# Two raw halves of a gate weight: landing place and place in the load queue

## The chip, the cores and the metric

The kernel runs on one core of a Trainium2 chip. A core has five engines that work side by side, each through its own instructions in order: TensorE (PE, matmuls), VectorE (DVE), ScalarE (ACT), GpSimd (POOL) and SyncE (SP, which here issues nearly all DMAs). They wait for each other through semaphores. The metric is the device time of one execution in microseconds, as the median of several runs.

## The reference, cut to what matters

One layer of an encoder: 1024 tokens of 1024 channels. The normalized input `h` is projected to queries, keys and values for two attention branches and to 2048 gate columns; each branch is projected to 1024 channels, gated, merged and projected again, and a SwiGLU block follows. The part of interest is the gate projection, and the last two units of the neighbourhood attention beside it:

```python
proj = h @ w_in[l]
qa, ka, va, qb, kb, vb, gates = jnp.split(proj, split_at, axis=-1)
...
o_a = neighbourhood_attention(qa, ka, va, rpb[l])
...
gate_a, gate_b = jnp.split(jax.nn.sigmoid(gates + b_gate[l]), 2, axis=-1)
merged = gate_a * (o_a @ w_proj_a[l]) + gate_b * (o_b @ w_proj_b[l])
```

## The kernel before

**Splitting.** Matmuls of float32 quality are made of three passes. `wsplit` (L125) makes a rounded upper part `whi` on ACT (L129) and the rest `wlo` on POOL or DVE (L130); each product then takes `whi` with both parts of the other operand and `wlo` with the upper part (`PASS`, L148).

**The gate products.** The gate columns are cut into eight weights `i`, each with four quarters of 128x512 (`q` = 0 to 3; in the text 5q3 is quarter 3 of weight 5). Products of 2x2 blocks are saved by mixing: with quarters w11, w12, w21, w22 (`q` 0 to 3), `x1 = w21 + w22`, `x2 = x1 - w11` and `x4 = w12 - x2` are formed on DVE (L761, L763, L768) and multiplied with mixed blocks of `h` that were prepared earlier. Weights go in pairs, `GPAIRS` = (5,6), (7,2), (0,1), (3,4), through four phases w11, w12, x1, x4 (`GPHASE`). One phase of one pair fills one slot `n` of the main loop: pair (5,6) the slots 80 to 83, pair (7,2) from 84 on. A phase has eight chunks of three matmuls (L773): four for the first weight of the pair, then attention work of the slot (scores L502, value products L543, transposes L528), then four for the second weight. What a product gives is drained from its `ps_d` bank, of which there are two, by L779 or L781 into `ga` and `gc` tiles and stored to DRAM (L808).

**Preparing a pair.** `gate_prep(p, part)` runs in the slots of `GPREP`: (0, 0) in slot 77, (0, 1) in slot 79. Part 0 splits quarters 0 and 1, part 1 mixes. Pairs behind the first are loaded whole by `gate_load` (L740) into a tile that a unit's queries and keys leave free. For the first pair no such tile is free, and its eight quarters go one by one through `wload` (L118) into the `raw` landing tiles of 128x512, of which there are six (`NRAW`). Quarters 0 and 1 of both weights hold four of them until they are mixed; the other two pass through the combine steps (`ut`, L677, read at L709 and L711).

**What sets the order.** PE's order is the program's. On ACT, DVE, POOL and SP a planner places the instructions: it simulates the program in time and takes, of what is ready, the first by program order, so DVE and the others then run in a fixed order on the chip. A tile with several buffers takes whichever is free in that simulation. `pin` (L113) keeps an instruction behind the one that was traced before it on its engine. `wload` with `keep` is pinned: in part 1 the loads of weight 6 are so pinned behind the store of weight 5's `x2` (L765).

**The attention tiles.** `big` (L162) gives one of eight tiles of 128x1024 (`NBIG`). At this point of the program they hold the bias tables of units 8 and 9 (two each, L449, read at L516), the values `v` of a unit (L378, loaded at L392), the weights of the conditioning rows (L296, read at L322), the accumulator `oacc` (L676, stored at L1104) and the gate's `gc` (L799).

```python
754                     gwt[i, nm] = wsplit(graw[i, q])
...
757         for i in pr:
758             for q in (2, 3) if p == 0 else ():
759                 graw[i, q] = gate_raw(i, q)
760             r = [graw.pop((i, q)) for q in range(4)]
761             nc.vector.tensor_add(r[2], r[2], r[3])
762             gwt[i, "x1"] = wsplit(r[2])
```

Of the kernel before, what the change touches and what calls it, by code (L numbers as in the profile page):

```python
# [48 lines left out]
def hybrid_layer(ctx: ExitStack, tc: tile.TileContext, x, colp, wada1, wada2, bada2, wqkv, wg, wpa, wpb,  # L49
                 wo, w1, w2, hgain, ropeg, rope, rbias, bmask, g2r, out):  # L50
    nc = tc.nc
# [61 lines left out]
    pin = tc.keep_in_program_order  # L113
# [4 lines left out]
    def wload(src, n, keep=False):  # L118
        raw = wp.tile([128, 512], F32, tag="raw", bufs=NRAW, name="raw")
        d = nc.sync.dma_start(raw[:, :n], src)  # L120
        if keep:
            tc.keep_in_program_order(d)
        return raw[:, :n]

    def wsplit(r, eng=None):  # L125
        n = r.shape[1]
        hi = wp.tile([128, 512], F32R, tag="hi", bufs=NHL, name="whi")
        lo = wp.tile([128, 512], F32R, tag="lo", bufs=NHL, name="wlo")
        nc.scalar.activation(hi[:, :n], r, AF.Copy)  # L129
        (eng or nc.gpsimd).tensor_sub(lo[:, :n], r, fview(hi[:, :n]))  # L130
        return hi, lo
# [30 lines left out]
    def big(name, shape=None, dtype=F32):  # L162
        return ap_.tile(shape or wide, dtype, tag="big", bufs=NBIG, name=name)
# [561 lines left out]
    gwt, gacc, gbank, graw, glate = {}, {}, {}, {}, {}  # L725
# [11 lines left out]
    def gate_raw(i, q):  # L737
        return wload(wg[i, :, 4 * q:4 * q + 4, :], 512, True)
# [8 lines left out]
    def gate_prep(p, part):  # L747
        pr = GPAIRS[p]
        if part == 0:
            for i in pr if p == 0 else ():  # L750
                for q in (0, 1):
                    graw[i, q] = gate_raw(i, q)
            for nm, q in (("w11", 0), ("w12", 1)):
                for i in pr:
                    gwt[i, nm] = wsplit(graw[i, q])
            return
        for i in pr:
            for q in (2, 3) if p == 0 else ():
                graw[i, q] = gate_raw(i, q)
            r = [graw.pop((i, q)) for q in range(4)]  # L760
            nc.vector.tensor_add(r[2], r[2], r[3])  # L761
            gwt[i, "x1"] = wsplit(r[2])
            nc.vector.tensor_sub(r[2], r[2], r[0])  # L763
            if p < 3:
                nc.sync.dma_start(sig_d[i, 4], r[2])  # L765
            else:
                glate[i] = r[2], r[3]
            nc.vector.tensor_sub(r[1], r[1], r[2])  # L768
            gwt[i, "x4"] = wsplit(r[1], nc.vector)
# [236 lines left out]
    for n in range(6, 92):  # L1006
# [92 lines left out]
        if n in GPREP:  # L1099
            gate_prep(*GPREP[n])  # L1100
# [152 lines left out]
    for i in GPAIRS[3]:  # L1253
        gacc[i] = [sig_half()]
        sig[i, 0, 0] = gacc[i][0]
        gate_acc(i, False)
    gate_prep(3, 1)
    cover("w11")
    mixed_load("x2")
# [493 lines left out]
```

## Time and profile before

| | |
|---|---|
| median of 3 runs | 1496.59 us (1496.54 to 1497.46) |
| the profiled execution | 1494.47 us |
| its span, first to last instruction | 1492.7 us |
| mean granted clock of TensorE | 0.998 |
| HBM read, written | 184.06 MB, 64.86 MB |

The profile is of one execution. Its page gives the busy time of each engine, and the trace behind it answers finer questions: who waited for whom, a timeline of each engine, busy time and granted clock in a stretch. In a timeline row stand the start, the duration, the engine, the line, the operation with output and input tiles, a count of merged instructions, and in brackets the idle time before it and what ended it. `PEld` is the weight load that overlaps matmuls, `SPq` a DMA issue by SP. The slots 80 to 83 of the loop, the four phases of the first gate pair, lie between about 512 and 550 us of the span.

### The profile page before, as it was taken

The page shows a single profiled execution, that of the slowest core. Times are in us where ns is not written, and L with a number is a line of the kernel's source. Part 1 is how long each engine was busy: PE and PEld are TensorE (multiplying, and loading weights), DVE is VectorE, ACT ScalarE, POOL GpSimd, SP SyncE. Part 2 cuts the span into 40 slices and gives each one's busy share as a digit, 9 for nine tenths or more (in the row PEclk, how much of TensorE's full clock was granted, in tenths as well). Part 3 has the DMA queues.
Part 4 walks back from the last instruction along what each step waited for, and adds up shares of the span by engine and source line. Part 5 has one row for each costly group of instructions (what it writes and reads, how often), then busy time and mean ns, then how long its engine had stood idle before and what let it go on. Part 6 is the DMA issues. An engine that isn't in the chain of part 4 may idle for free. (4 is left out here: it accounts for less than half of the span.)

```text
span 1492.7 us, 24300 instructions
## 1 busy us (share of the span) xinstructions
PE 1473.4 (99%) x8168; PEld 1260.0 (84%) x8168; DVE 1074.1 (72%) x2202; ACT 700.4 (47%) x1775; POOL 591.9 (40%) x580
## 2 busy tenths in 40 slices
PE   9999999999999989999999999999999999999998
PEld 7999998989898867888888888888888888887886
DVE  6877767667768854485765596888777777598468
ACT  5655665556776655465422353323223333354442
POOL 0342342242100122256431402677777775204464
PEclk9999999999999999999999999999999999999999
DMA  9725454576144454773452335345533334898342
GB/s 357 263 73 166 155 164 146 181 243 204 56 138 136 154 198 150 265 291 116 133 192 85 99 92 184 123 144 167 177 106 106 109 107 151 282 369 280 99 155 99
DMA packets 156908, 250.54 MB, mean 168 GB/s; under 512 B 26832, under 2 KB 70512, under 8 KB 156016
## 3 DMA queue, kind: packets, MB, share of 16 engines
q1 hardware_dynamic: 138208, 235.35, 47.0%
q10 hardware_dynamic: 18576, 13.64, 2.8%
q8 instruction: 65, 1.06, 0.3%
q14 instruction: 59, 0.48, 0.1%
HBM read 184.06 MB, written 64.86 MB: 167 GB/s over the span
## 5 line engine op out<-in xcount | busy, mean ns | idle before, releaser
L333 PE MATMUL ps_d<-whi,hT 128*128 128x384 f32 x1152 | 310.2, 340 | 1.6 <-ACT vs L371 0.8
L129 ACT ACTIVATE whi<-raw 128x512 fp32r<-128x512 f32 (+2 forms) x314 | 182.6, 594 | 210.7 <-PE ps_t L1588 33.5
L130 POOL TENSOR_TENSOR wlo<-raw,whi 128x512 fp32r<-128x512 f32 (+2 forms) x123 | 159.9, 1307 | 288.2 <-ACT whi L129 251.9
L130 DVE TENSOR_TENSOR wlo<-raw,whi 128x512 fp32r<-128x512 f32 (+1 forms) x191 | 167.9, 894 | 62.3 <-ACT whi L129 57.0
L333 PEld LDWEIGHTS ps_d<-whi,hT 128*128 128x128 f32 x1152 | 209.2, 188 | 3.6 <-ACT vs L371 1.2
L333 PE MATMUL ps_d<-wlo,hT 128*128 128x384 f32 x576 | 193.0, 335 | 0.8 <-POOL wlo L130 0.6
L333 PEld LDWEIGHTS ps_d<-wlo,hT 128*128 128x128 f32 x576 | 108.4, 188 | 1.3 <-POOL wlo L130 1.3
L129 ACT ACTIVATE whi<-ws 128x512 fp32r<-128x512 f32 x60 | 37.7, 628 | 119.5 <-DVE ws L1435 85.2
L1368 POOL TENSOR_TENSOR e<-e,c 128x512 f32<-128x512 f32 x44 | 68.5, 1556 | 60.6 <-DVE c L1498 36.5
L773 PE MATMUL ps_d<-hT,whi 128*128 128x512 f32 x256 | 81.4, 399 | 3.4 <-ACT whi L129 3.4
L363 POOL TENSOR_TENSOR ra<-qn,rtab 128x64 f32<-128x64 f32 x48 | 17.6, 367 | 142.8 <-DVE qn L356 121.0
L130 POOL TENSOR_TENSOR wlo<-m,whi 128x512 fp32r<-128x512 f32 x35 | 51.9, 1493 | 53.6 <-ACT whi L129 53.6
L1366 ACT ACTIVATE e<-e 128x512 f32<-128x512 f32 x44 | 27.4, 630 | 89.2 <-DVE e L1501 60.7
L130 POOL TENSOR_TENSOR wlo<-gl,whi 128x512 fp32r<-128x512 f32 x26 | 35.4, 1377 | 73.2 <-ACT whi L129 73.2
L581 ACT ACTIVATE P<-P,st 128x256 f32<-128x256 f32 (+2 forms) x100 | 45.7, 458 | 34.1 <-DVE st L579 33.9
L1418 PE MATMUL ps_v<-h2T,whi 128*128 128x512 f32 x192 | 59.2, 390 | 0.0
L1418 PE MATMUL ps_s<-h2T,whi 128*128 128x512 f32 x192 | 59.1, 389 | 0.0
L773 PEld LDWEIGHTS ps_d<-hT,whi 128*128 128x128 f32 x256 | 47.9, 191 | 13.1 <-ACT whi L129 3.6
L1418 PE MATMUL ps_d<-h2T,whi 128*128 128x512 f32 x184 | 56.7, 390 | 0.0
L1367 DVE TENSOR_TENSOR e<-e 128x512 f32<-128x512 f32 x44 | 42.9, 981 | 17.9 <-ACT e L1366 17.8
L140 ACT ACTIVATE ry<-ss,eps 128x4 f32<-128x4 f32 (+1 forms) x88 | 26.2, 298 | 61.1 <-DVE ss L354 45.1
L517 ACT ACTIVATE P<-P,sx 128x384 f32<-128x384 f32 (+1 forms) x64 | 37.2, 582 | 34.3 <-DVE sx L516 34.1
(411 smaller groups left out, 4052.5 us busy)
## 6 DMA issues: line engine op xcount, KB each, us to landing
raw<-in_w_dram SPq DMA_DIRECT2D x139, 256.0 KB, 3.2
ga_d<-e SPq DMA_DIRECT2D x77, 256.0 KB, 2.0
raw<-ga_d SPq DMA_DIRECT2D x77, 256.0 KB, 2.6
wa<-in_wada_dram SPq DMA_DIRECT2D x32, 512.0 KB, 5.3
raw<-in_wqkv_dram SPq DMA_DIRECT2D x80, 192.0 KB, 4.9
m<-in_w_dram SPq DMA_DIRECT2D x44, 256.0 KB, 5.1
xt<-in_x_dram SPq DMA_DIRECT2D x16, 512.0 KB, 4.2
land<-in_wada_dram SPq DMA_DIRECT2D x16, 512.0 KB, 9.3
```

The source lines that it names most:

```text
L129: nc.scalar.activation(hi[:, :n], r, AF.Copy)
L130: (eng or nc.gpsimd).tensor_sub(lo[:, :n], r, fview(hi[:, :n]))
L140: nc.scalar.activation(y, ss, AF.Ln, scale=1.0 / n, bias=eps)
L333: nc.tensor.matmul(pd[:, :384], tok(a, k, t), U.w[k][b][:, :384], start=(k == 0 and i == 0), stop=(k == KT - 1 and i == 2))
L363: nc.gpsimd.tensor_tensor(v4(ra), v4(qn[:, :, 0:16]), tv(0, 0, 16), op=ALU.mult)
L517: nc.scalar.activation(P[:nq, :nk], P[:nq, :nk], AF.Exp, scale=-1.0, bias=nm, accum_out=sm)
L581: nc.scalar.activation(C.P[h][:nq, c], C.P[h][:nq, c], AF.Exp, scale=-1.0, bias=nm, accum_out=sm)
L773: nc.tensor.matmul(pb, w[x][:, k * 128:(k + 1) * 128], b[y][:, k], start=(k == 0 and q == 0), stop=(k == 3 and q == 2))
L1366: nc.scalar.activation(sg, a, AF.Sigmoid)
L1367: nc.vector.tensor_mul(sg, sg, a)
L1368: nc.gpsimd.tensor_mul(sg, sg, up)
L1418: nc.tensor.matmul(pb, w[p][:, k * 128:(k + 1) * 128], b[q][:, k], start=(k == 0 and i == 0), stop=(k == 3 and i == 2))
```

## The change

In part 1 of the first pair, the four loads of quarters 2 and 3 are taken out of the loop over the two weights and put ahead of it, in the order 5q2, 5q3, 6q2, 6q3. Weight 5's quarters go to `raw` tiles as before. Weight 6's go to the two halves of a new attention tile `wgx`, by two DMAs that are pinned too. The mixing is as before.

```diff
             return
+        if p == 0:
+            z = big("wgx")
+            for i in pr:
+                for q in (2, 3):
+                    graw[i, q] = gate_raw(i, q) if i == pr[0] else z[:, 512 * q - 1024:512 * q - 512]
+            for q in (2, 3):
+                pin(nc.sync.dma_start(graw[pr[1], q], wg[pr[1], :, 4 * q:4 * q + 4, :]))
         for i in pr:
-            for q in (2, 3) if p == 0 else ():
-                graw[i, q] = gate_raw(i, q)
             r = [graw.pop((i, q)) for q in range(4)]
             nc.vector.tensor_add(r[2], r[2], r[3])
             gwt[i, "x1"] = wsplit(r[2])
```

## The prediction

> **What bounds the kernel now.** I read the page first, then the waits of PE, then the timelines of PE, SP, DVE and POOL around the one long wait. In the fences "5" and "6" are the two weights of the first gate pair, "5q3" is the fourth quarter of weight 5, and `L773` is the gate's matmul line.
>
> ```profile
> span 1492.7 us, 24300 instructions
> PE 1473.4 (99%) x8168; PEld 1260.0 (84%) x8168; DVE 1074.1 (72%) x2202; ACT 700.4 (47%) x1775; POOL 591.9 (40%) x580
> PE ps_d L773 <- ACT whi L129: 3.4, 1, 3.4
> PE ps_d L773 <- POOL wlo L130: 1.1, 2, 0.6
> PE ps_v L403 <- POOL qn L366: 2.7, 3, 1.3
> PE ps_d L1588 <- DVE wlo L130: 1.7, 3, 1.2
> ```
>
> PE is busy for 1473.4 of 1492.7 us, so nothing that shortens another engine's work can help unless it ends a wait of PE, and all such waits together are 19.3 us. Of the waits (total, times, longest) the first is the longest single one in the program, 3.4 us in front of one gate matmul; the second stands beside it. The last row is also all that is left behind 545 us. Here is the place, on PE:
>
> ```profile
> 528.85 0.62 PE L773 MATMUL ps_d<-hT,whi 128*128 128x512 f32 x2
> 529.90 0.50 PE L773 MATMUL ps_d<-hT,wlo 128*128 128x512 f32 x1 [0.43 <-POOL wlo L130]
> 533.74 0.66 PE L528 MATMUL ps_t<-ident,P 128*128 128x128 f32 x4
> 537.79 0.73 PE L773 MATMUL ps_d<-hT,whi 128*128 128x512 f32 x2 [3.39 <-ACT whi L129]
> 539.15 0.80 PE L773 MATMUL ps_d<-hT,wlo 128*128 128x512 f32 x1 [0.63 <-POOL wlo L130]
> 543.10 0.61 PE L773 MATMUL ps_d<-hT,whi 128*128 128x512 f32 x2
> 547.21 0.66 PE L528 MATMUL ps_t<-ident,P 128*128 128x128 f32 x4
> 547.62 0.71 PE L773 MATMUL ps_d<-hT,whi 128*128 128x512 f32 x2
> 550.46 0.62 PE L773 MATMUL ps_d<-hT,whi 128*128 128x512 f32 x2
> 537.70:543.10 5.40, 4.68 (x13) 3.46 (x14) 2.42 (x6) 2.47 (x8) 1.28 (x1) 0.68 1.00 409
> 547.60:550.40 2.80, 2.80 (x15) 2.34 (x14) 1.01 (x6) 2.48 (x8) 2.59 (x3) 1.00 0.31 112
> ```
>
> The product of 5's mixed weight starts at 528.85, that of 6 at 537.79, after the wait. The two last rows are windows (length, busy of PE, PEld, DVE, ACT, POOL, then the granted clock): behind the wait PE works at 0.68 of its clock, while the same twelve matmuls one phase later have 1.00. So the stop is paid twice, once as idle time and once as slow matmuls. Why weight 6 is late stands on SP, DVE and POOL:
>
> ```profile
> 522.32 0.33 SPq L120 DMA_DIRECT2D raw<-in_wg_dram  x1
> 522.76 0.40 SPq L392 DMA_DIRECT2D v<-v_d  x1
> 530.60 0.32 SPq L765 DMA_DIRECT2D sig_d<-raw  x1
> 531.01 0.88 SPq L120 DMA_DIRECT2D raw<-in_wg_dram  x2
> 532.41 0.95 SPq L743 DMA_DIRECT2D gl<-in_wg_dram  x2
> 521.20 1.09 DVE L711 TENSOR_TENSOR ps_t<-ut,ps_t 128x512 f32<-128x512 f32 x1 [0.32 <-PE ps_t L701]
> 527.12 0.69 DVE L761 TENSOR_TENSOR raw<-raw 128x512 f32<-128x512 f32 x1 [2.18 <-issue]
> 529.88 0.69 DVE L763 TENSOR_TENSOR raw<-raw 128x512 f32<-128x512 f32 x1 [0.28 <-POOL wlo L130]
> 536.32 0.69 DVE L761 TENSOR_TENSOR raw<-raw 128x512 f32<-128x512 f32 x1 [2.85 <-DMA raw<-in_wg_dram]
> 528.56 1.29 POOL L130 TENSOR_TENSOR wlo<-raw,whi 128x512 fp32r<-128x512 f32 x1 [19.27 <-ACT whi L129]
> 537.81 1.28 POOL L130 TENSOR_TENSOR wlo<-raw,whi 128x512 fp32r<-128x512 f32 x1 [7.97 <-ACT whi L129]
> ```
>
> 5q3 is issued when the combine step's multiply at 521.20 gives its landing tile back (522.3) and is added at 527.12, 4.8 us after its issue. 6q2 and 6q3 are pinned behind the store of 5's difference (530.60), which needs the subtraction at 529.88. So they go out at 531.01, are there for the add at 536.32, and the upper part of the sum reaches PE 1.47 us later (537.79), the lower part 2.83 us later (539.15).
>
> **The change part by part.** It adds and removes no instruction of PE, DVE, ACT or POOL and no byte of DMA; four things move.
>
> 1. *The two loads go ahead.* All four loads of the halves are pinned in a row, so 6q2 and 6q3 stand right behind 5q3. At the spacing of the pair at 531.01 (0.88 us for two) they are issued at 522.7 and 523.1. In the trace the add came 4.9 us after the issue of the later one of the pair (536.32 less 531.45): landing at 528.0. If the 512 KB queue against 5q3 and the v load as well, 512 KB at the 409 GB/s of the window above are 1.3 us more: 529.3. The add, the copy and the subtraction put the upper part at 529.5 to 530.8 and the lower at 530.9 to 532.2; POOL is free from 529.85.
>
> 2. *What PE then finds.* Behind four transposes the next product follows 0.41 us after their start (547.21 to 547.62), so 6's product could start at 534.15, and its first `wlo` matmul 0.62 us later (528.85 to 529.90, less the wait of 0.43). Both parts are there 2.5 us or more before. The gain is 537.79 - 534.15 = 3.64 us, and of the twelve matmuls the excess over the same twelve at full clock, (543.10 - 537.79) - (550.46 - 547.62) = 5.31 - 2.84 = 2.47 us, of which 0.63 is the second wait and 1.84 the clock. **Sum: 6.1 us.**
>
> The Trainium skill ("TensorE: Matmul & The Clock Gate", What's actually happening) says that the array falls to half its clock after an idle window of about 3.4 us and needs as long a busy one to come back; 3.4 us at half rate would be an estimated 1.7 us lost instead of 1.84, and the sum 6.0. The granted clock of 0.68 behind the 3.39 us wait agrees.
>
> 3. *5's own product.* 5q3 keeps its issue, so the 0.43 us wait at 529.90 stays. If the loads behind it share the engines with it, it lands up to 1.3 us later and PE waits that much longer: cost 0 to 1.3 us. I take 0, because v's 512 KB stand right behind it today too (522.76) and it landed in 4.8 us, no later than the pair at 531.01 with little queued between.
>
> The Trainium skill ("DMA: Bandwidth & Descriptors", Queues, rings and completion order) speaks against that: descriptors of one queue are started in order, yet a later transfer may finish its writes before an earlier one. By the order nothing is lost and the sum is 6.1; by free overtaking it would be an estimated 4.8.
>
> 4. *The attention tile.* There are eight. The rows that show who holds them:
>
> ```profile
> 487.66 0.75 DVE L322 SCALAR_TENSOR_TENSOR acc<-wa,cact,acc 128x512 f32<-128x512 f32 x1
> 523.91 0.69 DVE L781 TENSOR_TENSOR gc<-ga,ps_d 128x512 f32<-128x512 f32 x1 [0.90 <-PE ps_d L773]
> 524.51 0.42 DVE L516 CUSTOM_DVE_ANT_0 P<-ps_s,rb 128x256 f32<-128x256 f32 x1
> 527.73 0.42 DVE L516 CUSTOM_DVE_ANT_0 P<-ps_s,rb 128x256 f32<-128x256 f32 x1
> 533.41 0.85 SPq L1104 DMA_DIRECT2D o_d<-oacc  x1
> 546.62 0.66 PE L543 MATMUL ps_v<-PT,v 128*64 128x128 f32 x8
> ```
>
> At 522.7 six are in use: two bias tables of unit 8 (read last at 524.51 and 527.73), two of unit 9, the `v` of unit 8 (read until 546.62) and `oacc` (stored at 533.41). The last two ada tiles are free since 488.4; today the `v` of unit 9 (522.76) and the gate's `gc` (523.91) take them. Afterwards the new tile and `v` do, and `gc` must wait for the first bias table: its add comes at 524.9 at the earliest, not at 523.91. It empties a `ps_d` bank that 5's product needs at 528.85. Behind the bias step alone that costs nothing; behind 5's add it ends at 527.8 + 0.69 = 528.5, still nothing; behind both adds (527.1 and 529.3) at 530.0 + 0.69 = 530.7, where PE waits 1.85 us, 1.4 more than the 0.43 it waits anyway. Bounds 0 to 1.4 us; I take 0, as the bias step at 524.51 frees the tile 2.6 us before the first add can start.
>
> **What is late next.** Everything behind moves up by 6.1 us. The next loads are the 2 MB of pair two (532.41), held by the drain of 6's product of 525.9 to 528.85 and its store, not by the moved loads; they only lose 512 KB in front of them.
>
> ```profile
> 542.76 0.62 ACT L129 ACTIVATE whi<-gl 128x512 fp32r<-128x512 f32 x1
> 543.45 6.73 POOL L130 TENSOR_TENSOR wlo<-gl,whi 128x512 fp32r<-128x512 f32 x5 [4.36 <-ACT whi L129]
> ```
>
> Their first product would go from 550.46 to 544.35 and wants the upper part by then and the lower by 544.97. Today the copy ends at 543.38 and the lower part at 543.45 + 1.35 = 544.80. So even unmoved they come just in time; if they slipped, PE would pay all but 0.2 us. The `v` load behind the two raws loses 0.9 us and is first read two phases later. Behind 545 us the waits of PE sum to 1.7 us; a new order by the planner can shift such waits, and I allow 1.7 us either way.
>
> **Forecast.** The profiled execution took 1494.47 us (span 1492.7); 6.1 less is 1488.4. It lies 2.1 us under the median of the runs, 1496.59, and the time that counts is the median: 1496.59 - 6.1 = **1490.5 us** (-0.41%). About 0.2% (3.0 us) is what a measurement of this kernel can tell from no change.
>
> **The rivals.**
> - *Shared late.* The 512 KB delay 5q3, or `gc` stands behind both adds: 1.3 to 1.4 us of the 6.1 are given back, 1491.9. For it: four transfers in place of two between 522.3 and 524. Against: as in 3 and 4.
> - *The loads are not early, or the add isn't.* If no tile is free at 522.7, the loads go out after the bias step at 527.73 (528.2 and 528.6), land at 533.5, upper part 535.0, lower 536.3: PE waits 0.85 and 0.7 us, with no loss of clock: gain 4.6, 1492.0. The same comes out if the planner leaves 6's add behind the first bias step after 533.0. If it lands from 535 on, the gain is under 3.0: no change, 1493.6 to 1499.6. Against: two tiles were demonstrably free.
> - *A stop in a new place, slower.* DVE works in order. If 6's add stands before the `gc` add and its load is late, PE stops at 528.85 until landing + 1.4 us. With the clock loss of 1.84 the gain of 6.1 is used up at a stop of 4.3 us, that is at a landing at 531.7, and 3.0 us are lost at 534.7, 11.6 us after issue: 1499.6 or more. For it: 1 MB loads take up to 10.6 us here.
>
> ```profile
> gl<-in_wg_dram SPq DMA_DIRECT2D x2, 1024.0 KB, 10.6
> raw<-in_w_dram SPq DMA_DIRECT2D x139, 256.0 KB, 3.2
> ```
>
>   Against: a 256 KB load takes a median of 3.2 us, and the queue at 522 holds 1.3 MB, not 2.5.
>
> **Chances.** Forecast (gain 6.1 with the 1.7 us either way, 1488.8 to 1492.2) 0.62; shared late 0.08 and late add 0.10, both still faster; no change 0.13; slower 0.07. Faster is 0.62 + 0.08 + 0.10 = 0.80. To hold the time 8 times in 10 the forecast's range is stretched to the two faster rivals with the same 1.7 us on top: 1488.8 to 1493.6.
>
> **What would show it.** SP: four raw loads of the gate in a row near 514 and 522 to 523. DVE: both adds before 531. PE: no wait on `whi` between 533 and 538, clock 1.00 there, 6's product about 0.4 us behind the transposes, and the 0.43 us wait still there. I am wrong if PE waits in front of 5's product, or if the `gc` add stands behind a load, or if the gate's next pairs get waits that aren't there today.

## The result and the profile after

| | before | after |
|---|---|---|
| median | 1496.7 us (1496.49 to 1498.01, 6 runs) | 1491.72 us (1489.16 to 1494.49, 6 runs) |
| ratio of after to before | | 0.9965, 95% interval 0.9953 to 0.9978 |
| the profiled execution | 1494.47 us | 1494.49 us |
| its span | 1492.7 us | 1492.7 us |
| start of the gate's first matmul in it | 511.86 us | 517.06 us |
| from there to the first w11 matmul of weight 2 | 43.34 us | 38.42 us |

The changed kernel is 5.0 us faster by the medians. The two profiled executions, though, have the same span. The last two rows explain that: the execution of the changed kernel that was profiled came to the gate 5.2 us later, and then needed 4.9 us less for the gate's first nine products. In front of the gate both programs are alike in the order of every engine, so the late start is no effect of the change; two runs below test that. In what follows the gate's stretch is read by itself, from the first matmul of the gate to the first of w11 of weight 2. Lines behind 756 are moved by 5 in the changed kernel: L778 is the gate's matmul, L766 the first add of the mixing, L786 the `gc` add.

The page of the profile after, and four of the waits of PE over the whole span (total, times, longest):

```profile
span 1492.7 us, 24299 instructions
PE 1474.4 (99%) x8168; PEld 1260.7 (84%) x8168; DVE 1073.9 (72%) x2202; ACT 700.6 (47%) x1775; POOL 592.5 (40%) x580
```

```profile
PE ps_v L403 <- POOL qn L366: 3.2, 4, 1.3
PE ps_d L333 <- ACT whi L129: 1.4, 1, 1.4
PE ps_d L778 <- DVE gc L786: 0.8, 1, 0.8
PE ps_d L778 <- POOL wlo L130: 0.5, 1, 0.5
```

The 3.4 us wait on `whi` at the gate is gone. A wait on `wlo` is left, and one on the `gc` drain is new. PE's timeline at the place, with 5's x1 product (534.05), 6's (538.63) and the next two phases:

```profile
534.05 0.61 PE L778 MATMUL ps_d<-hT,whi 128*128 128x512 f32 x2
538.22 0.66 PE L528 MATMUL ps_t<-ident,P 128*128 128x128 f32 x4
538.63 0.71 PE L778 MATMUL ps_d<-hT,whi 128*128 128x512 f32 x2
539.87 0.50 PE L778 MATMUL ps_d<-hT,wlo 128*128 128x512 f32 x1 [0.53 <-POOL wlo L130]
542.31 0.62 PE L778 MATMUL ps_d<-hT,whi 128*128 128x512 f32 x2
546.84 0.71 PE L778 MATMUL ps_d<-hT,whi 128*128 128x512 f32 x2
550.61 0.73 PE L778 MATMUL ps_d<-hT,whi 128*128 128x512 f32 x2 [0.77 <-DVE gc L786]
```

6's product follows 0.41 us behind its transposes, and its twelve matmuls take 3.68 us (538.63 to 542.31) where they took 5.31. The window over them shows the granted clock, last but two, back at 1.00:

```profile
538.60:542.30 3.70, 3.17 (x15) 2.29 (x14) 2.50 (x10) 2.70 (x9) 1.22 (x1) 1.00 0.95 321
```

SP's timeline, then the instructions of DVE, ACT and POOL that answer to those of before:

```profile
527.53 0.33 SPq L120 DMA_DIRECT2D raw<-in_wg_dram  x1
527.91 0.92 SPq L763 DMA_DIRECT2D wgx<-in_wg_dram  x2
528.93 0.38 SPq L392 DMA_DIRECT2D v<-v_d  x1
538.31 0.89 SPq L743 DMA_DIRECT2D gl<-in_wg_dram  x2
```

```profile
531.50 0.69 DVE L766 TENSOR_TENSOR raw<-raw 128x512 f32<-128x512 f32 x1 [1.41 <-issue]
532.45 0.68 DVE L786 TENSOR_TENSOR gc<-ga,ps_d 128x512 f32<-128x512 f32 x1
533.13 1.65 DVE L766 TENSOR_TENSOR wgx<-wgx 128x512 f32<-128x512 f32 x1
549.26 0.69 DVE L766 TENSOR_TENSOR gl<-gl 128x512 f32<-128x512 f32 x1 [3.26 <-DMA gl<-in_wg_dram]
549.87 0.68 DVE L786 TENSOR_TENSOR gc<-gc,ps_d 128x512 f32<-128x512 f32 x1
```

```profile
537.31 0.63 ACT L129 ACTIVATE whi<-raw 128x512 fp32r<-128x512 f32 x1 [0.80 <-DVE raw L773]
537.84 0.62 ACT L129 ACTIVATE whi<-wgx 128x512 fp32r<-128x512 f32 x1
```

The loads go out as the change says, right behind 5q3, and 6's add starts 5.6 us after 5q3's issue instead of 14.0. Two things stand out. 6's sum is finished at 534.78 (533.13 + 1.65), but ACT splits it only at 537.84, behind the split of 5's x4, which waits for DVE: from there come the 0.53 us. And at 549.26 DVE waits 3.26 us for the second 1 MB load of pair two, with the `gc` add behind it; PE wants that bank and waits 0.77 us.

### The profile page after: what moved, and what is told of

It reads as the page before. It is cut to its first block, busy times and chain, and to the rows that moved or that the text cites. A ratio compares the mean times of both kernels' runs of the same rounds, so it can differ in the third digit from the quotient of the medians.

```text
span 1492.7 us, 24299 instructions
## 1 busy us (share of the span) xinstructions
PE 1474.4 (99%) x8168; PEld 1260.7 (84%) x8168; DVE 1073.9 (72%) x2202; ACT 700.6 (47%) x1775; POOL 592.5 (40%) x580
## 3 DMA queue, kind: packets, MB, share of 16 engines
q8 instruction: 65, 1.06, 0.3%
## 5 line engine op out<-in xcount | busy, mean ns | idle before, releaser
L778 PE MATMUL ps_d<-hT,whi 128*128 128x512 f32 x256 | 80.5, 396 | 0.8 <-DVE gc L786 0.8
L130 POOL TENSOR_TENSOR wlo<-m,whi 128x512 fp32r<-128x512 f32 x35 | 51.4, 1480 | 54.5 <-ACT whi L129 54.5
L778 PEld LDWEIGHTS ps_d<-hT,whi 128*128 128x128 f32 x256 | 46.9, 188 | 10.6 <-DVE gc L786 1.2
L143 DVE TENSOR_TENSOR rz<-ry,rv 128x4 f32<-128x4 f32 (+1 forms) x88 | 27.6, 314 | 34.1 <-ACT ry L142 33.2
```

The costliest lines, as they stand in the source:

```text
L143: nc.vector.tensor_mul(z, y, v)
L778: nc.tensor.matmul(pb, w[x][:, k * 128:(k + 1) * 128], b[y][:, k], start=(k == 0 and q == 0), stop=(k == 3 and q == 2))
```

## The experiments

Each kernel is compared with runs of the kernel before that were taken beside it: median 1497.43 us (28 runs) for before_again, after_again, tile_only and place_only, 1497.34 (16) for warm_fill, sums_first, add_late and sums_late, 1497.06 (14) for the other three. The table gives the gate's stretch from PE's timelines: "first" is the start of the gate's first matmul, the next four columns are differences of starts.

| kernel | first | 5's x1 to 6's x1 | 6's x1 to 5's x4 | 5's x4 to w11 of 7 | first to w11 of 2 | ratio to before, interval |
|---|---|---|---|---|---|---|
| before | 511.86 | 8.94 | 5.31 | 7.36 | 43.34 | |
| before_again | 513.20 | 8.73 | 5.33 | 7.39 | 43.18 | 1.0001 (0.9992 to 1.0009) |
| after | 517.06 | 4.58 | 3.68 | 8.30 | 38.42 | 0.9965 (0.9953 to 0.9978) |
| after_again | 515.26 | 4.58 | 3.72 | 7.37 | 37.42 | 0.9965 (0.9952 to 0.9978) |
| after_third | 512.67 | 4.60 | 3.72 | 7.77 | 37.98 | 0.9959 (0.9946 to 0.9972) |
| tile_only | 513.85 | 6.33 | 5.26 | 7.45 | 42.60 | 0.9985 (0.9976 to 0.9993) |
| place_only | 514.15 | 6.62 | 3.76 | 7.36 | 39.48 | 0.9979 (0.9970 to 0.9987) |
| warm_fill | 511.93 | 8.51 | 3.76 | 7.37 | 41.38 | 0.9998 (0.9987 to 1.0008) |
| warm_fill_2 | 516.45 | 9.09 | 3.75 | 7.36 | 41.94 | 0.9997 (0.9984 to 1.0010) |
| sums_first | 513.35 | 4.57 | 2.83 | 8.42 | 38.17 | 0.9967 (0.9954 to 0.9979) |
| add_late | 514.36 | 4.58 | 3.61 | 7.36 | 37.28 | 0.9962 (0.9950 to 0.9975) |
| sums_late | 513.57 | 4.58 | 2.82 | 7.91 | 37.04 | 0.9954 (0.9942 to 0.9967) |
| sums_late_2 | 513.07 | 4.83 | 2.85 | 7.57 | 36.98 | 0.9954 (0.9941 to 0.9967) |

### Both kernels as they are

No edit; the question is where the 5.2 us in front of the gate come from.

> The kernel before, unchanged. Theory that the early part of the program (before 500 us, where both kernels are alike in every engine's order) varies by itself between executions: its own profile reaches the gate's first matmul up to 5 us earlier or later than the 511.9 us of the profile before, with or without half-clock stretches near 196 and 263 us, and the times spread over some us. Rival, that the change made the early part vary: time 1496.7 within 0.8 us, gate reached at 511.9 within 0.5 us.

> The changed kernel, unchanged. Early part varies by itself: gate reached somewhere between 511.9 and 517.1 us, and from the gate's first matmul to the end 5.0 to 5.5 us less than before, whatever the early part took; median 1490.5 to 1492. Rival, that the change slows the early part: gate reached near 517 us again.

The kernel before took 1493.83 to 1499.45 us in its 28 runs, the changed one 1489.53 to 1494.2 in 5. In thirteen profiles the gate's first matmul starts between 511.86 and 517.06 us, for kernels of both kinds. So the early part varies by itself, and the changed kernel's own profile had the latest start of all. Part of it is the clock. The same window of the trace, before and after, with the granted clock last but two:

```profile
196.00:200.00 4.00, 4.00 (x25) 4.00 (x24) 1.12 (x6) 2.31 (x7) 0.00 (x0) 1.00 0.06 16
```

```profile
196.00:200.00 4.00, 4.00 (x16) 4.00 (x15) 1.55 (x6) 1.94 (x8) 0.00 (x0) 0.57 0.09 33
```

The order is the same; one execution did 25 matmuls in these 4 us, the other 16. The profile after has a second such stretch at 264.55 us. Each lasts 3.41 us at half clock, so the two lost an estimated 3.4 of the 5.2 us; ten of the thirteen profiles have none in front of the gate. From the gate on, the changed kernel won 4.8, 5.8 and 5.3 us (its three whole stretches against the mean of before, 43.26): its gain is there in every profile, whatever the early part took.

### The tile without the place, the place without the tile

```diff
 # tile_only, on the kernel before
+        z = big("wgx") if p == 0 else None
         for i in pr:
             for q in (2, 3) if p == 0 else ():
-                graw[i, q] = gate_raw(i, q)
+                if i == pr[0]:
+                    graw[i, q] = gate_raw(i, q)
+                else:
+                    graw[i, q] = z[:, 512 * q - 1024:512 * q - 512]
+                    pin(nc.sync.dma_start(graw[i, q], wg[i, :, 4 * q:4 * q + 4, :]))
 # place_only, on the kernel before
-        for i in pr:
-            for q in (2, 3) if p == 0 else ():
-                graw[i, q] = gate_raw(i, q)
+        if p == 0:
+            for i in pr:
+                for q in (2, 3):
+                    graw[i, q] = gate_raw(i, q)
+        for i in pr:
```

> Weight 6's quarters 2 and 3 land in the attention tile, but their loads stay in the loop, pinned behind the store of weight 5's difference. Theory (the place in the queue holds them): issued 0.4 us behind that store as before, the 3.4 us wait of PE and the half clock behind it stay, 1496.7 within 1 us. Rival (the landing tiles hold them): the loads go out by 528 us in the time of the profile before, the wait is gone, 1491 to 1492.

> All four loads ahead of the mixing, but weight 6's quarters land in raw tiles like weight 5's. Theory (both the place and the tile are needed): with six raw tiles 6q2 gets the tile of 5q3 after weight 5's add (527.8 in the time before) and 6q3 one after the subtraction (530.6), so it lands at 535.4 in place of 536.3 and the wait is 2.5 us: 0.9 us gained if the clock still falls, 2.7 if it doesn't, 1494.0 to 1495.8. Rival (the place alone does it): 1491 to 1492.

tile_only measured 1495.4 us, place_only 1493.4. SP, PE and DVE of tile_only (its lines are those of the changed kernel), and the window over 6's product:

```profile
524.31 0.33 SPq L120 DMA_DIRECT2D raw<-in_wg_dram  x1
531.27 0.32 SPq L770 DMA_DIRECT2D sig_d<-raw  x1
531.65 0.93 SPq L764 DMA_DIRECT2D wgx<-in_wg_dram  x2
```

```profile
532.67 0.70 PE L778 MATMUL ps_d<-hT,whi 128*128 128x512 f32 x2 [1.67 <-ACT whi L129]
539.00 0.73 PE L778 MATMUL ps_d<-hT,whi 128*128 128x512 f32 x2 [1.38 <-ACT whi L129]
```

```profile
527.79 0.69 DVE L766 TENSOR_TENSOR raw<-raw 128x512 f32<-128x512 f32 x1 [0.91 <-issue]
531.89 0.68 DVE L786 TENSOR_TENSOR gc<-ga,ps_d 128x512 f32<-128x512 f32 x1
```

```profile
539.00:544.20 5.20, 4.58 (x12) 3.37 (x13) 3.05 (x7) 3.90 (x11) 1.80 (x2) 0.69 1.01 420
```

The loads stay 0.4 us behind the store, and the stop is split rather than removed: 1.67 us in front of 5's product and 1.38 in front of 6's, with the half clock behind it. The first is put down to ACT, whose split was long done (529.1); what ended last is the `gc` add, which had to drain the bank and ended at 531.89 + 0.68 = 532.57. `gc` and `v` (532.67) both come only behind the `wgx` loads (531.65), though by the count in point 4 of the prediction two tiles were free: it looks as if the tiles are given out in the order of the program, so that both wait for `wgx` to take its own, but no run shows that. Point 4 priced a late tile; the reason here is another. The gate gains 0.7 us by the profile; the median says 2.0, more than that place can explain, and what gives the rest was not found.

place_only does most of the work alone. The loads go out as raw tiles come free, 6q2 at 530.14 and 6q3 at 532.89 (of the store no more); PE's timeline and the window of 6's product:

```profile
537.76 0.73 PE L775 MATMUL ps_d<-hT,whi 128*128 128x512 f32 x2 [1.06 <-ACT whi L129]
539.12 0.50 PE L775 MATMUL ps_d<-hT,wlo 128*128 128x512 f32 x1 [0.63 <-POOL wlo L130]
```

```profile
537.70:541.60 3.90, 3.21 (x13) 2.36 (x14) 2.03 (x5) 2.85 (x10) 1.28 (x1) 1.00 0.94 300
```

The wait is 1.06 us in place of 3.39, the clock stays, and the gate needs 39.48 us: 3.8 of the 5.3 us that the change gains on average. Its expectation was 0.9 to 2.7. The second load goes out only 0.9 us earlier against 5's product than before (1.75 in place of 2.64 us behind its start), as expected; but its add follows 3.4 us after the issue in place of 4.8, so that the sum comes 2.3 us earlier. Why the load was faster no run shows; the 2 MB of pair two stand 1.7 us behind it in place of 0.9. So the theory that both parts are needed holds only for the rest; without a tile the place alone gave the larger part.

### The clock by itself

```diff
 # warm_fill and warm_fill_2, on the kernel before, in gate_pre
+            if n == 2 and c == 4:
+                pw = bank("v")
+                for m in range(9):
+                    nc.tensor.matmul(pw, gwt[GPAIRS[0][0], "x1"][0][:, :128], hT[0][:, 0, :512], start=True, stop=True)
             if k == 0:
                 gbank[i] = bank("d")
```

> The kernel before, with nine more matmuls of 128x512 in PE's order just ahead of weight 6's x1 product; their result is not used. They fit in the 3.6 us that PE waits there (nine times 0.23 us is 2.1 us). Theory that the second part of the loss, 1.84 us, is the clock and falls because PE stands idle: the wait of PE shrinks to about 1.5 us, the twelve matmuls behind it take 3.5 us from the start of the first to the start of the next product in place of 5.3, granted clock 1.00 there; from the gate's first matmul to the first of w11 of weight 2 41.5 us in place of 43.3. Rival, that the clock falls whatever PE does there (for the 400 GB/s of loads, say): 5.3 us and 43.3 us as before.

> The kernel with the nine filling matmuls once more. Theory: its first profile kept the clock at the gate (41.4 us from the gate's first matmul to the first of w11 of weight 2, against 43.3), and lost 4.9 us near 1365 us, where every engine's order is that of the kernel before, by chance; so the gate takes 41.4 us again, the loss near 1365 us is under 1 us, and the median is 1 to 2 us under the kernel before. Rival, the filling costs something later: the loss near 1365 us is there again.

```profile
534.13 2.33 PE L794 MATMUL ps_v<-hT,whi 128*128 128x512 f32 x9
537.43 0.73 PE L773 MATMUL ps_d<-hT,whi 128*128 128x512 f32 x2 [0.97 <-ACT whi L129]
```

```profile
537.40:541.20 3.80, 3.15 (x13) 2.29 (x14) 1.85 (x4) 1.53 (x5) 1.28 (x1) 1.00 0.99 411
```

6's sum comes about as late as before (added at 535.96, before at 536.32), DMA runs at 411 GB/s (before 409), and only PE is kept busy for 2.3 of the 3.3 us in front of the product: the clock stays at 1.00 and the product takes 3.76 and 3.75 us instead of 5.31. So this part of the loss, some 1.6 us, is the clock, and it falls for want of matmuls. The medians (1496.96 and 1498.49 us) don't show the gain; the intervals don't exclude it either. In the first profile PE lost it again in front of the last matmul stage, with the clock at half from 1366.95 to 1370.37, where every engine's order is that of before:

```profile
PE ps_d L1592 <- DVE wlo L130: 2.7, 4, 2.0
PE ps_d L1592 <- ACT whi L129: 1.7, 1, 1.7
```

The second profile had less there (2.5 and 0.2 us, 1.3 us lost against before around 1347 to 1365), more than the 1 us that was expected. Whether the filling costs something later or these executions met that by chance is not settled.

### The two waits that were left

```diff
 # sums_first, on the changed kernel
         for i in pr:
-            r = [graw.pop((i, q)) for q in range(4)]
+            r = [graw[i, q] for q in range(4)]
             nc.vector.tensor_add(r[2], r[2], r[3])
             gwt[i, "x1"] = wsplit(r[2])
+        for i in pr:
+            r = [graw.pop((i, q)) for q in range(4)]
 # add_late, on the changed kernel
-            nc.vector.tensor_add(r[2], r[2], r[3])
+            s = nc.vector.tensor_add(r[2], r[2], r[3])
+            if p > 0:
+                pin(s)
 # sums_late and sums_late_2: both
```

> The changed kernel with the loop over the two weights cut in two: both x1 sums and their splits first, then the rest of the mixing of both. Theory: the 0.5 us wait of PE for the lower part of weight 6's x1 comes from ACT's order, where the upper part of weight 5's x4 stands ahead of it; it goes, and from the gate's first matmul to the first of w11 of weight 2 it takes 36.8 us in place of 37.4, or 37.6 if the wait on the gc drain comes up. Rival, POOL or the landing is what is late: 37.4 or more, with the wait on wlo still there.

> The changed kernel with pair two's (and later pairs') first add pinned behind what is traced before it on DVE. Theory: the 0.8 us wait of PE for the gc drain in the profile after comes from that add, which stands ahead of the drain on DVE and waits for the 1 MB load; pinned, the drain comes first, no wait on gc, 37.4 us from the gate's first matmul to the first of w11 of weight 2. Rival, the wait is on the load through the split of w11 as well: a wait of PE on whi or wlo takes its place.

> Both of the last two edits on the changed kernel. If they act one by one: no wait on wlo at weight 6's x1 and none on gc, 36.8 us from the gate's first matmul to the first of w11 of weight 2, median 0.6 to 1.2 us under the changed kernel's, 1490.2 to 1491. Rival, one order disturbs the other: 37.4 us or more.

> The changed kernel with both edits once more: 36.8 to 37.1 us from the gate's first matmul to the first of w11 of weight 2, and a median of 1489.5 to 1491, under the changed kernel's 1491.2 to 1491.7. Rival, the 1490.0 was chance: 1491.2 or more.

> The changed kernel once more, on the same chip as the two beside it: 37.4 us at the gate, or 38.4 if the wait on the gc drain comes up; median 1491 to 1492.

The waits of PE at the gate, of sums_first, add_late and sums_late (there L780 and L782 are the gate's matmul, L786 and L788 the copy by ACT into `gc`; the second line is at transposes in the same stretch):

```profile
PE ps_d L780 <- ACT gc L786: 0.8, 1, 0.8
PE ps_t L528 <- ACT P L520: 0.4, 1, 0.4
```

```profile
PE ps_d L780 <- POOL wlo L130: 0.5, 1, 0.5
```

```profile
PE ps_d L782 <- ACT gc L788: 0.3, 1, 0.3
```

With the sums first, 6's product takes 2.83 us, as at full speed: the 0.53 us wait came from ACT's order, and with what follows it (a weight load of 0.19 us that no matmul covers is part of that) it cost 0.85 us. In that profile other waits came in its place: 0.8 us, as ACT's `gc` copy (542.66) stood behind a split (542.12) that waited 2.62 us for pair two's load, and 0.4 us at the transposes. So the gate took 38.17 us, over the 36.8 or 37.6 that were expected. With the add pinned, the wait on DVE's `gc` add is gone (5's x4 to w11 of 7: 7.36) and the one on `wlo` is left; after_again had no wait on `gc` without the pin either, so one profile doesn't prove the pin. With both, the gate takes 37.04 and 36.98 us, and the medians are 1490.0 and 1490.45 us against 1491.55 of the changed kernel beside the second. This is the fastest version found. By the intervals, 0.9954 (0.9941 to 0.9967) beside 0.9959 (0.9946 to 0.9972), the runs can't tell it from the changed kernel; the gate's stretch does.

## Why the prediction was right

The forecast was 1490.5 us, 6.1 less than before; measured were 1491.72, 1491.23 and 1491.55, 5.0 to 6.2 less than the kernel before beside them. The main terms of the sum, the idle time and the clock, held. That the total came so close is luck in part, as misses on both sides offset each other. Point by point:

1. *The loads go ahead.* Right. They were issued 0.4 and 0.8 us behind 5q3, and 6's add started 5.6 us after 5q3's issue, against a forecast landing after 5.7 to 7.0.
2. *What PE then finds.* The idle time of 3.64 us went as worked out, 0.41 us between the transposes and the product. Of the 2.47 us on the twelve matmuls, 1.6 went. The other 0.85 is the mis-sized term: the forecast let the second wait (0.63) go, as the lower part would be ready by 532.2 at the latest. DVE had the sum in time; ACT's order, which the forecast never worked out, held it.
3. *5's own product.* The cost was taken as 0, with 5q3's landing unchanged. It was better than that: 5q3's add came 3.97 us after its issue, not 4.80, and the 0.43 us wait went; between 5's x1 and 6's x1 4.3 us were saved (mean of before 8.84, after 4.58), 0.6 more than the 3.64. The rows suggest why. Where the `v` load stands right behind 5q3 (the kernel before, place_only and the two with the filling), 5q3's add comes 4.7 to 4.8 us after issue; with 6's raw loads behind it 3.8 to 4.1 us (seven profiles); in tile_only, where `v` goes out 8.4 us later and nothing follows for 7 us, 3.5 us (524.31 to 527.79). So a load seems to be delayed by what stands behind it; no run changed that and nothing else. The Trainium skill ("DMA: Bandwidth & Descriptors", Queues, rings and completion order) says that a later transfer may finish its writes before an earlier one. Whether one did no row shows, but the rows agree so far that the order of issue didn't shield the load. The loss that the prediction drew from it had the wrong sign here, since the change moves `v` further back.
4. *The attention tile.* Right in the cost of 0, not in the order: the forecast put `gc` behind the first bias step and ahead of 5's add. It came behind both bias steps and 5's add, and the bank was empty at 533.13, 0.9 us ahead of the product that needs it. tile_only shows what a late `gc` costs: 1.67 us.
5. *What is late next.* The forecast had the loads of pair two "just in time" and said it would be wrong if the `gc` add stood behind a load. It did: 0.8, 0 and 0.2 us in three profiles. That, and the 0.85 us of point 2, are what the measured gain lacks; the 0.6 us of point 3 is what it has on top. 4.3 + 1.6 = 5.9, less 0 to 0.9, is 5.0 to 5.9, against the 4.8 to 5.8 us of the gate's stretch.

Of the rivals, neither a delayed 5q3 nor late loads nor a stop in front of 5's product came up. The clock was priced by the row (1.84) and by the Trainium skill ("TensorE: Matmul & The Clock Gate", What's actually happening: an idle window of about 3.4 us). Both sizes fit the 1.6 us of the runs. The condition is another: in tile_only the clock stayed at 1.00 for 8 us behind the stop of 1.67 us and fell at 541.00, behind stops of 1.38 and 0.62 us, while in warm_fill_2 stops of 1.47 and 0.62 us left it at 1.00. So no single stop has to reach 3.4 us, and its length alone doesn't decide; the last section has what the traces show of it.

## What to carry to other kernels

A wait of a few microseconds in front of one matmul can cost half as much again in clock; read the window behind it before pricing it. When loads are held both by a landing tile and by a place in a queue, try the place alone first: here it brought 3.8 of 5.3 us without a tile. And when a change removes a wait, follow the freed value through every engine up to PE, and ask which instruction now stands behind the next load.

## What the runs showed of the hardware

- Executions of one program differ by over 5 us in places that no engine's order explains: 1493.83 to 1499.45 us for the kernel before. Two profiled executions with one span can hide a change of 5 us; a stretch measured from the first matmul that the change can touch does not.
- In the thirteen traces the granted clock is 1.00 or 0.50 between 10 and 1480 us. It fell eight times, and each time it stayed at 0.50 for 3.41 us (before: 539.11 to 542.52) or, once, for twice that (warm_fill_2: 261.88 to 268.71). The two falls in the profile after lie 68.26 us apart, 20 times 3.41.
- Each trace can be cut into stretches of 3.41 us, counted from the first rise of its clock. Then every fall comes at the end of a stretch. In seven of the eight, PE had been idle for 1.90 to 2.68 us of that stretch, in one stop or in two; of the stretches without a fall, the most idle one had 1.86 us. The eighth fall (profile after, 196.29) came behind only 1.26 us and is not explained.
- So it matters where a stop lies in these stretches, and that changes between executions. tile_only's 1.38 and 0.62 us lie in one (537.59 to 541.00); warm_fill_2's 1.47 and 0.62 us lie in two, of which the fuller holds 1.37. Near 261 us, stops of 1.38 and 0.64 us cost the clock in the profile after and not in sums_late. The 1.06 and 0.63 us of place_only are less than 1.86 even together.
- An add of two 128x512 tiles on DVE took 1.65 us at 533.13, beside a POOL subtraction from 532.94 to 534.23; such an add with POOL idle took 0.69 us (531.50). In all seven profiles with 6's loads ahead in `wgx`, 6's add ran beside that subtraction and took 1.64 to 1.66 us.
